# Storing three outputs of a 90-degree rotation in two halves each

## The chip, the cores and the metric

The kernel runs on one core of one Trainium2 chip. The metric is the device time of one execution in microseconds. The experiments were run in four groups on three chips, so each is set against the runs of the kernel before in its own group. "Before" and "changed" are the two kernels; where a time is quoted, it is the median of the runs.

## The reference

```python
def setup_inputs():
    return {"x": np.random.randn(8192, 8192).astype(np.float32), "k": 1}

def reference(x, k):
    return np.rot90(x, k)
```

Nothing is computed. 268 MB are read, turned by a quarter, and 268 MB are written.

## The kernel before

The input is cut into macro tiles of 1024 rows by 4096 columns. A macro tile is read by eight loads of 2 MB (128 rows each). VectorE (DVE) reverses the order of the elements inside blocks of 128, TensorE (PE) transposes 128x128 blocks into PSUM, ScalarE (ACT) copies PSUM into an output tile, and the output tile is stored (2 MB). One output needs two PSUM tiles, so two copies. There are two input buffers (`a`), two output buffers (`o`, shared with the first loads), and 68 small buffers between DVE and PE. Loads are issued by SP, stores by ACT. The last of the 16 macro tiles is cut in two tiles of 512 rows each (four loads and four outputs of 2 MB apiece), and the eight loads of these two come before their stores in the program.

```python
    def load(r0, rt, c0):
        for t in range(rt):
            ...  # a = a tile of a_pool (two buffers); some of the first eight in o_pool
            loads += 1
            nc.sync.dma_start(
                out=a[:], in_=x[r0 + t * P : r0 + (t + 1) * P, c0 : c0 + W]
            )
            ...  # eight DVE copies into tiles of r_pool (68 buffers)

    def store(r0, rt, c0, chunks, end):
        ...  # G = 4 column blocks in one output (8 in the last two tiles), PW = G / 2 in one PSUM tile
        for i, g0 in enumerate(range(0, W // P, G)):
            ...  # ot = a tile of o_pool (two buffers); in the last two tiles every other one of a_pool
            o = ot[:, : G * rows].rearrange("m (g f) -> m g f", g=G)
            S = PW if end and r0 + rows == N and g0 + G == W // P else G
            for h in range(0, G, PW):
                ...  # transposes into ps
                nc.scalar.copy(o[:, G - PW - h : G - h, :], ps)
                done = h + PW
                if done % S == 0:
                    top = M - c0 - (g0 + done) * P
                    dst = out[top : top + S * P, r0 : r0 + rows].rearrange(
                        "(g m) f -> m g f", g=S
                    )
                    nc.scalar.dma_start(out=dst, in_=o[:, G - done : G - done + S, :])
```

`S` says how many column blocks one store takes: all of the output, or half of it. Before, only the very last output is stored in halves. Numbering the outputs from 1, those of the whole macro tiles are 1 to 120, those of the last macro tile but one 121 to 124, the last ones 125 to 128.

## Time and profile before

| before | |
|---|---|
| time | 1267.97 us (6 runs, 1267.50 to 1268.66) |
| moved | 537 MB, 425 GB/s on average, 427 to 430 in most slices |
| busy | PE 55%, ACT 37%, DVE 28% |
| one store every | 9.8 us in mid run |

The first lines are from the page of the kernel before. Part 2 gives 40 slices of the span; part 3 gives for each DMA queue its packets, MB and share of the engines (q1 carries the loads, q10 the stores); part 4 is the chain of waits; part 6 lists the DMA issues with their size and time to landing.

```profile
span 1266.0 us, 10386 instructions
...
DMA  9999999999999999999999999999999999999998
GB/s 398 416 431 429 429 428 429 430 427 430 427 429 429 429 429 430 428 429 428 430 428 428 429 429 427 427 429 426 430 429 427 414 428 430 426 427 428 428 393 370
...
q10 hardware_dynamic: 18576, 268.44, 50.0%
q1 hardware_dynamic: 18432, 268.44, 49.9%
...
DMA out_dram<-ot 74%; ACT ot L147 19%; DMA a<-in_x_dram 3%; DVE ar L106 1%; ACTq L155 0%; PE pt L142 0%; ACTq L147 0%; DVEq L106 0%
...
out_dram<-ot ACTq DMA_DIRECT2D x127, 2048.0 KB, 15.9
```

The DMA is full from end to end (9 tenths or more in 39 of 40 slices). The chain names the stores, but a store takes 15.9 us to land while both queues share 428 GB/s; the first 2 MB loads, with no stores beside them, landed 4.9 us apart. No slice of the page is above 431 GB/s.

The timeline of the kernel before where the first stores start (start us, length us, engine, line, operation; ACTq is the issue of a DMA on ACT's queue, x2 are two of a kind in a row; in brackets the idle time before and what ended it):

```profile
49.65 0.65 ACTq L155 DMA_DIRECT2D out_dram<-ot  x1
...
54.16 0.55 ACTq L155 DMA_DIRECT2D out_dram<-ot  x1
...
60.89 3.64 ACT L147 COPY ot<-pt 128x2048 f32<-128x2048 f32 x2 [6.75 <-DMA out_dram<-ot]
...
64.55 0.55 ACTq L155 DMA_DIRECT2D out_dram<-ot  x1
```

The third output has to wait until the first store has landed (60.89 us), because there are two output buffers.

The same, near the end; the store at 1215.46 is that of output 120:

```profile
1205.62 0.55 ACTq L155 DMA_DIRECT2D out_dram<-ot  x1
1211.80 3.63 ACT L147 COPY ot<-pt 128x2048 f32<-128x2048 f32 x2 [6.21 <-DMA out_dram<-ot]
1215.46 0.55 ACTq L155 DMA_DIRECT2D out_dram<-ot  x1
```

The kernel before in stretches of 4 and 2 us (the last two columns are the DMA share and GB/s; in so short a stretch the figure is rough, and single ones come out above the 431 GB/s of the fullest slice of the page):

```profile
1208.00:1212.00 4.00, 2.48 (x14) 2.24 (x12) 2.77 (x8) 0.20 (x1) 0.00 (x0) 0.77 0.99 422
1212.00:1214.00 2.00, 0.28 (x2) 0.28 (x3) 0.00 (x0) 2.00 (x2) 0.00 (x0) 0.82 1.03 430
1214.00:1216.00 2.00, 2.00 (x11) 2.00 (x11) 0.00 (x0) 1.43 (x1) 0.00 (x0) 0.50 0.29 123
1216.00:1218.00 2.00, 2.00 (x17) 2.00 (x16) 0.02 (x1) 0.86 (x1) 0.00 (x0) 0.83 0.89 377
1218.00:1220.00 2.00, 1.78 (x17) 1.54 (x15) 2.00 (x6) 2.00 (x2) 0.00 (x0) 1.00 1.01 426
1220.00:1222.00 2.00, 2.00 (x21) 1.96 (x20) 0.76 (x3) 1.33 (x2) 0.00 (x0) 1.00 0.66 279
```

There is one idle stretch after 1214 us, until the store of 1215.46 starts to move, and a small one at 1221.5.

### The profile page before, as it was taken

Reading aid. Unit: us, or ns where it says so; the run is one execution under the profiler, and the core shown is the slowest. Engines: PE = TensorE matmul, PEld = TensorE weight load, DVE = VectorE, ACT = ScalarE, POOL = GpSimd, SP = SyncE. Lnnn points to the kernel's source line nnn. Section 1 sums busy time; section 2 is a strip of 40 time slices with the busy share of each in tenths; the row PEclk is TensorE's granted clock in tenths of the full one; section 3 lists DMA queues with packets and bytes.
Section 4 is the critical chain, followed back from the end, with each engine's and each line's share of the span. In section 5 each row is a group of like instructions: output and inputs, shape, how many; then the busy total and the mean of one; then the engine's idle time right before and its main releaser. Section 6 shows DMA issues by size and latency. Waiting matters only on the chain.

```text
span 1266.0 us, 10386 instructions
## 1 busy us (share of the span) xinstructions
PE 700.4 (55%) x4096; PEld 660.8 (52%) x4096; DVE 354.9 (28%) x1024; ACT 467.3 (37%) x257; POOL 0.7 (0%) x6
## 2 busy tenths in 40 slices
PE   1456455665655555555556546565464665656573
PEld 0355455554545455554555445464464654556573
DVE  4422322232222322233222322233222332223210
ACT  0333334333433334333433334333433334333364
POOL 0000000000000000000000000000000000000000
PEclk9986777777678777787777877778777667777687
DMA  9999999999999999999999999999999999999998
GB/s 398 416 431 429 429 428 429 430 427 430 427 429 429 429 429 430 428 429 428 430 428 428 429 429 427 427 429 426 430 429 427 414 428 430 426 427 428 428 393 370
DMA packets 37057, 537.55 MB, mean 425 GB/s; under 512 B 4112, under 2 KB 4112, under 8 KB 4112
## 3 DMA queue, kind: packets, MB, share of 16 engines
q10 hardware_dynamic: 18576, 268.44, 50.0%
q1 hardware_dynamic: 18432, 268.44, 49.9%
q8 instruction: 32, 0.52, 0.2%
q14 instruction: 17, 0.14, 0.0%
HBM read 268.44 MB, written 268.44 MB: 424 GB/s over the span
## 4 chain that ended last, share of the span: by engine, by line
DMA 78%; ACT 19%; issue 1%; DVE 1%; ACTq 0%; PE 0%; DVEq 0%
DMA out_dram<-ot 74%; ACT ot L147 19%; DMA a<-in_x_dram 3%; DVE ar L106 1%; ACTq L155 0%; PE pt L142 0%; ACTq L147 0%; DVEq L106 0%
## 5 line engine op out<-in xcount | busy, mean ns | idle before, releaser
L142 PE MATMUL pt<-ident,ar 128*128 128x128 f32 x4096 | 700.4, 350 | 548.3 <-ACT ot L147 465.9
L142 PEld LDWEIGHTS pt<-ident,ar 128*128 128x128 f32 x4096 | 660.8, 187 | 587.7 <-ACT ot L147 496.4
L147 ACT COPY ot<-pt 128x2048 f32<-128x2048 f32 x256 | 466.0, 1869 | 742.6 <-DMA out_dram<-ot 729.5
L106 DVE COPY ar<-a 128x512 f32<-128x512 f32 x1024 | 354.9, 420 | 865.8 <-DMA a<-in_x_dram 811.4
L147 ACT ACT_TABLE_LOAD x1 | 1.3, 1283 | 41.1 <-DVE ar L106 41.1
masks.py:199 POOL TENSOR_SCALAR_AFFINE_SELECT ident<-ident 128x128 f32<-128x128 f32 x1 | 0.3, 294 | 0.1
masks.py:197 POOL MEMSET ident<- 128x128 f32 x1 | 0.2, 205 | 0.3 <-POOLq L184 0.3
L184 POOL MEMSET const-bfloat16-1.0<- 128x1 bf16 x1 | 0.1, 102 | 0.0
L184 POOL MEMSET const-uint8-127<- 128x1 uint8 x1 | 0.1, 102 | 0.0
L184 POOL MEMSET const-float32-0.0<- 128x1 f32 x1 | 0.1, 99 | 0.2 <-issue 0.2
L184 POOL MEMSET const-float32-1.0<- 128x1 f32 x1 | 0.1, 99 | 0.0
## 6 DMA issues: line engine op xcount, KB each, us to landing
a<-in_x_dram SPq DMA_DIRECT2D x128, 2048.0 KB, 16.8
out_dram<-ot ACTq DMA_DIRECT2D x127, 2048.0 KB, 15.9
out_dram<-ot ACTq DMA_DIRECT2D x2, 1024.0 KB, 13.7
```

The lines of the kernel that those rows point to most:

```text
L106: nc.vector.tensor_copy(out=ar[:], in_=a[:, j * CH : (j + 1) * CH].rearrange("r (b m) -> r b m", m=P)[:, :, ::-1],)
L142: nc.tensor.transpose(ps[:, PW - 1 - w, t * P : (t + 1) * P], chunks[t, g * P // CH][:, g % (CH // P), :], ident,)
L147: nc.scalar.copy(o[:, G - PW - h : G - h, :], ps)
L184: nc = _bacc.Bacc("TRN2", target_bir_lowering=False, num_devices=1)
```

## The change

The intent is to let the DMA have stores sooner: the first two outputs of the first macro tile, and the first output of the last macro tile but one (outputs 1, 2 and 121), are stored in two halves, the first of them as soon as the first of the two copies is done.

```diff
-            S = PW if end and r0 + rows == N and g0 + G == W // P else G
+            starts = r0 == 0 and c0 == 0 and i < 2 or end and r0 + rows < N and i == 0
+            ends = r0 + rows == N and c0 + W == M and g0 + G == W // P
+            S = PW if starts or ends else G
```

`ends` picks the same output as the old condition. Nothing else is changed.

## The prediction

> **What bounds the kernel.** The DMA. The page gives a DMA share of 9 tenths or more in 39 of 40 slices and 427 to 430 GB/s in nearly every slice[...]. PE 55%, ACT 37% and DVE 28% are no limits. The chain of waits is 74% "DMA out<-ot" and 19% ACT copy, but that loop of two output buffers closes at the pace of the full DMA: one store per 9.8 us is 4 MB moved at 428 GB/s. 537 MB at that rate take 1254 us. So about 12 us are ramp, gaps and tail, and only a gap in the DMA can be won.
>
> **Where the DMA loses time** (stretches of 0.5 to 2 us, and the packet records):
> - start, 0 to 6 us: about 3 us, not touched;
> - 54 to 61 us, when the first two stores start: the rate falls to 279, then about 400 GB/s, while all 16 engines count as busy; the usual 0.61 us packets take up to 1.3 us. Lost: about 0.9 us of every engine. Load 9 has just ended (51.3), load 10 was issued at 50.82 but moves only from 55.4, and the first store, issued at 49.65, is the only supply: a thin queue;
> - 1214 to 1216.5 us: most engines idle up to 2.6 us, until the store issued at 1215.46; 1221.4 to 1221.9: idle 0.3 to 0.5 us, until the one issued at 1220.82;
> - end: most engines finish at 1261.7 us, one lags to 1264.4.
>
> **What the change does.** Same bytes, copies and transposes; three more stores on ACT's queue, 0.55 us of issue each (timeline).
> 1. First macro tile: the first half (1 MB) is issued at about 47.8 instead of 49.65, the second at about 50.2. It shares the DMA with load 9, which lands 1 to 2 us later (nothing urgent waits for it). The queue is less thin at 51 to 56 us. If thinness causes the slow packets, up to 0.9 us comes back; otherwise nothing. The DMA was never idle there, so an earlier store by itself wins nothing.
> 2. Last macro tile but one: the first half goes out at about 1219.0 instead of 1220.82 and fills the gap at 1221.4. But the lagging engine, which ends last, has no gap there: it ends the store before at 1224.1 and goes straight on. Less idle time of the others does not move the end. The second half and the following stores go out 0.6 us later, which the DMA's backlog hides. Value: about 0.
> 3. The gap at 1214 belongs to the output before, which is not split. It stays.
> 4. Extra ACT issue time (under 2 us in total) is off the limit.
>
> **Prediction.** 0.7 us less: 1267.3 us, range 1265.3 to 1268.8. Faster by over 2%: 0.5%; within 2%: 99%; slower: 0.5%.
>
> **What would show it.** Step 1: stretches of 54 to 62 us above 410 GB/s, packets of 0.61 us. If they still show about 280 GB/s, step 1 is wrong. Step 2: no idle at 1221.5, yet the end still set by the lagging engine. Step 3: the fall at 1214 to 1216 us unchanged. Steady state: 9.8 us per store as before.
>
> **What would make it wrong.** If the earlier first stores leave loads and stores in another order for the whole run, the spread between the DMA engines (0.4 us at the first loads, 8.5 us at the last) may grow or shrink, and the end with it by 1 to 3 us. Or the half stores delay load 10 so that a real gap opens near 60 us.

## The result, and the profile after

| | before | changed |
|---|---|---|
| median (6 runs each) | 1267.97 us | 1269.79 us |
| lowest to highest | 1267.50 to 1268.66 | 1269.65 to 1270.37 |
| time of the profiled run | 1267.83 us | 1270.37 us |

The ratio is 1.0015 (95% interval 1.0002 to 1.0027). It is the mean time of the changed kernel's runs over the mean of the other's runs of the same rounds, so it is not quite the ratio of the medians. The change costs 1.8 us: far below 2%, but clear of the noise. The profiled run of the changed kernel was its slowest, so the two profiles differ by 2.5 us.

The page of the changed kernel:

```profile
span 1268.6 us, 10387 instructions
...
GB/s 399 423 423 429 429 429 429 429 428 429 428 429 430 428 429 428 428 428 427 428 428 425 428 428 429 428 426 427 428 428 426 427 428 424 428 427 427 429 356 371
...
q10 hardware_dynamic: 19008, 268.44, 49.9%
q1 hardware_dynamic: 18432, 268.44, 49.8%
...
out_dram<-ot ACTq DMA_DIRECT2D x8, 1024.0 KB, 13.7
```

Mid run is the same. The slices that fall most are the 39th (393 to 356 GB/s), near 1220 us, and the third (431 to 423). The stores' queue has 432 more packets: each of the three outputs went out in twice as many packets of half the size, 8 KB in place of 16 KB (384 more; the other 48 are packets of 4 bytes, 16 for each store).

The timeline of the changed kernel at its first stores:

```profile
47.80 2.33 ACTq L157 DMA_DIRECT2D out_dram<-ot  x2
...
52.14 2.31 ACTq L157 DMA_DIRECT2D out_dram<-ot  x2
...
65.92 3.64 ACT L149 COPY ot<-pt 128x2048 f32<-128x2048 f32 x2 [12.04 <-DMA out_dram<-ot]
...
69.59 0.55 ACTq L157 DMA_DIRECT2D out_dram<-ot  x1
```

The first half was issued 1.85 us earlier (47.80 in place of 49.65), but the first output **landed 5 us later**: ACT may begin the third output at 65.92 us, before at 60.89.

Near the end of the changed kernel, with the store of output 120 now at 1218.78:

```profile
1210.77 0.55 ACTq L157 DMA_DIRECT2D out_dram<-ot  x1
1215.12 3.63 ACT L149 COPY ot<-pt 128x2048 f32<-128x2048 f32 x2 [4.38 <-DMA out_dram<-ot]
1218.78 0.55 ACTq L157 DMA_DIRECT2D out_dram<-ot  x1
```

The changed kernel in the same stretches:

```profile
1208.00:1212.00 4.00, 2.98 (x14) 2.98 (x15) 0.00 (x0) 2.74 (x2) 0.00 (x0) 0.50 0.48 205
1212.00:1214.00 2.00, 2.00 (x12) 2.00 (x11) 1.27 (x4) 0.00 (x0) 0.00 (x0) 0.50 1.11 467
1214.00:1216.00 2.00, 1.30 (x10) 1.06 (x9) 1.59 (x5) 0.88 (x1) 0.00 (x0) 0.92 0.94 401
1216.00:1218.00 2.00, 0.96 (x9) 0.97 (x10) 0.01 (x1) 2.00 (x2) 0.00 (x0) 1.00 0.39 164
1218.00:1220.00 2.00, 2.00 (x21) 1.96 (x19) 0.00 (x0) 1.30 (x2) 0.00 (x0) 1.00 0.12 49
1220.00:1222.00 2.00, 1.40 (x14) 1.17 (x12) 0.00 (x0) 2.00 (x2) 0.00 (x0) 1.00 1.17 492
```

There is a new hole from about 1216.7 to 1220 us, in which hardly any DMA engine works, besides an idle stretch before it (from 1208 to 1212 us the DMA share is 0.48; before it was 0.99). The packet records of the trace, which hold every packet of every queue, give the sums:

| from the packet records | before | changed |
|---|---|---|
| idle per DMA engine, 1200 to 1245 us | 2.17 us | 4.81 us |
| the last load lands (mean over the DMA engines) | 1211.8 us | 1206.6 us |
| the last packet of the run ends | 1265.1 us | 1267.6 us |
| loads minus stores, mean of 200 to 400 us | 19.8 MB | 22.1 MB |

The last row is the number of MB that the loads have moved minus those that the stores have moved; I call it the **lead** of the loads. (Here and in all runs below, a packet counts in proportion to the part of it that is done, and every trace is laid so that its first load packet starts at 2.24 us. In the timelines and stretches that packet starts at 1.75 us, so times from the packet records are about 0.5 us later than theirs.) The idle time grew by 2.64 us, and the profiled time by 2.54. That points to where the time is; it is no exact account, as e9 below shows. The lead tells when it was decided: it is 20.1 MB in both kernels at 50 us, and at 70 us it is 19.9 before and 21.7 in the changed kernel. After that it stays, in the changed kernel, for the whole run: 22.0 MB still at 1150 to 1199 us against 19.9.

So the loads get one load (2 MB) ahead of the stores in the first 25 us of stores. All loads are then done 5.2 us earlier (2.2 MB at 428 GB/s), and what is left for the last stretch is stores alone. There, as I read it, two output buffers can't feed the DMA: one store of 2 MB is gone in 4.9 us (an estimate: 2 MB at 428 GB/s), but the next has to wait for a buffer to land and for two copies of 1.87 us. Whether this hole is the loss is tested with e8.

### The profile page after: what moved, and what is told of

The parts are those of the page before. It is cut to its first block, busy times and chain, and to the rows that moved or that the text cites. A ratio compares the mean times of both kernels' runs of the same rounds, so it can differ in the third digit from the quotient of the medians.

```text
span 1268.6 us, 10387 instructions
## 1 busy us (share of the span) xinstructions
PE 714.5 (56%) x4096; PEld 680.9 (54%) x4096; DVE 364.5 (29%) x1024; ACT 466.6 (37%) x257; POOL 0.7 (0%) x6
## 4 chain that ended last, share of the span: by engine, by line
DMA 77%; ACT 20%; issue 1%; PE 1%; ACTq 0%; DVE 0%; SPq 0%
DMA out_dram<-ot 74%; ACT ot L149 20%; DMA a<-in_x_dram 3%; PE pt L144 1%; ACTq L157 0%; DVE ar L106 0%; ACTq L149 0%; SPq L101 0%
## 5 line engine op out<-in xcount | busy, mean ns | idle before, releaser
L144 PE MATMUL pt<-ident,ar 128*128 128x128 f32 x4096 | 714.5, 356 | 536.5 <-ACT ot L149 497.6
L144 PEld LDWEIGHTS pt<-ident,ar 128*128 128x128 f32 x4096 | 680.9, 191 | 569.8 <-ACT ot L149 527.7
L106 DVE COPY ar<-a 128x512 f32<-128x512 f32 x1024 | 364.5, 422 | 851.5 <-DMA a<-in_x_dram 719.6
```

The costliest lines, as they stand in the source:

```text
L106: nc.vector.tensor_copy(out=ar[:], in_=a[:, j * CH : (j + 1) * CH].rearrange("r (b m) -> r b m", m=P)[:, :, ::-1],)
L144: nc.tensor.transpose(ps[:, PW - 1 - w, t * P : (t + 1) * P], chunks[t, g * P // CH][:, g % (CH // P), :], ident,)
```

## The experiments

All runs gave correct results. Each was run in five rounds, of which one was profiled: leads, idle times and packet counts are of that one execution. (e1 and e9 start like the kernel before, and their leads came out within 0.3 MB of its own.) The kernel before ran nine times beside each group (medians 1267.94 to 1268.20 us).

**The theories.** A: the halves at the start give the loads their lead, and the lead costs the time at the end. C (rival): the split near the end costs it. Within A, two causes of the lead. A1: the DMA engines serve the two queues packet by packet; with 8 KB packets of stores against 16 KB packets of loads, the stores get one byte for two. A2: the earlier issue by itself changes the order.

A1 is so far a guess. Counting packets of both queues that start between 62 and 66 us shows whether it holds here:

| 62 to 66 us | load packets (size, GB/s) | store packets (size, GB/s) |
|---|---|---|
| before | 42 (16 KB, 172) | 62 (16 KB, 254) |
| changed | 64 (16 KB, 262) | 80 (8 KB, 164) |
| e2, start only | 73 (16 KB, 299) | 70 (8 KB, 143) |
| e4, small loads | 109 (8 KB, 223) | 100 (8 KB, 205) |
| e5, before with small loads | 72 (8 KB, 147) | 69 (16 KB, 283) |
| e6, late columns | 90 (16 KB, 369) | 92 (2 KB, 47) |

In the runs with halves the numbers of packets are equal within a quarter, whatever their sizes, from 8:1 to 1:2, and the bytes follow the sizes. In the kernel before they are not equal although the sizes are. The order of the packets tells more. The records don't name the DMA engine, but where a packet ends, another mostly starts within 5 ns; I take it to be the next one of that engine, and leave out the 8 to 35% where none or several fit. From 62 to 66 us the queue changed in 106 of 120 such steps in the changed kernel, 129 of 130 in e5, 119 of 119 in e6, and 74 of 85 in the kernel before; all 11 exceptions there were a store after a store, as if that engine had no load packet waiting, which was not shown. So here, between 62 and 66 us, the queues took turns packet by packet in 87 to 100% of these steps.

### Which of the splits? e1 and e2

e1 keeps the split near the end alone, e2 the two at the start alone:

```diff
# e1_end_only
+            starts = end and r0 + rows < N and i == 0
# e2_start_only
+            starts = r0 == 0 and c0 == 0 and i < 2
```

> Only the split in the last macro tile but one; the first macro tile as before. Theory A (the halves at the start let the loads run one load, about 2 MB, ahead of the stores, and this costs at the end): as before, 1268.0 us within 0.5; loads minus stores moved stays at 19.9 MB in mid run; the gap at 1221.5 us is filled but the end does not move. Theory C (the split near the end costs the time, by its extra store issues): about 1269.8 us, as the changed kernel.

> Only the two splits in the first macro tile; the end as before. Theory A: about 1269.8 us as the changed kernel (1269.3 to 1270.3), loads minus stores about 22 MB from 70 us to the end, and an idle stretch of about 3 us of all DMA engines near 1217 to 1220 us. Theory C: 1268.0 us.

e1: 1267.83 us, ratio 1.0000 (0.9987 to 1.0012), lead 20.1 MB, idle 2.41 us. e2: 1270.62 us (1269.54 to 1273.20), ratio 1.0022 (1.0009 to 1.0034), lead 22.0 MB, idle 4.43 us. Theory C falls. The split near the end neither wins nor costs anything that could be measured; the two at the start make the whole loss.

### A run that did not do what it should: e3

e3 should issue both halves after the second copy, to keep the small packets and take away the early issue:

```diff
+                if late and done < G:
+                    continue
+                for d in range(S, G + 1, S) if late else [done]:
                     ...  # the store of half d
```

> The first two outputs are stored in halves as in the changed kernel (8 KB packets), but both halves are issued after the second copy, so nothing is issued earlier than before; the end is not split. Theory A1 (it is the size of the store packets: 8 KB against 16 KB of the loads, so the loads move two bytes for one): loads minus stores still rises to about 22 MB and the time is 1269.3 to 1270.3 us. Theory A2 (it is the earlier issue that changes the order): loads minus stores stays near 19.9 MB and the time is 1268.0 us within 0.5.

It measured 1270.05 us (1269.78 to 1272.84) and a lead of 22.1 MB, but it tells nothing: the first half was still issued at 47.54 us. The order of the instructions was as written, but the first store did not wait for the second copy, which it does not read: ACT's queue issued it while that copy still ran (47.54 to 49.41 us):

```profile
47.54 2.44 ACTq L161 DMA_DIRECT2D out_dram<-ot  x2
```

It is a second run of e2, no more.

### Packet size against early issue: e4

e4 keeps the early halves, and makes the packets of the three loads beside them equally small, by splitting those loads (9 to 11, counted from 0; the counter has been raised by one at this place) into two halves of columns. The end is not split, so it is e2 with smaller load packets:

```diff
+            n = 2 if loads in (10, 11, 12) else 1
+            for b in range(n):
+                lo, hi = b * W // n, (b + 1) * W // n
                 nc.sync.dma_start(
-                out=a[:], in_=x[r0 + t * P : r0 + (t + 1) * P, c0 : c0 + W]
+                    out=a[:, lo:hi],
+                    in_=x[r0 + t * P : r0 + (t + 1) * P, c0 + lo : c0 + hi],
                 )
```

> The two splits at the start, and the three loads that share the DMA with them (numbers 9 to 11 from 0) are also issued in two halves of columns, so their packets are 8 KB too. The end is not split. Theory A1: the two kinds of packets are of one size again, loads minus stores comes back to about 20 MB and the time to 1268.0 us within 0.5. Theory A2: loads minus stores stays at 22 MB, the time at about 1269.8 us.

1268.63 us, ratio 1.0008 (0.9995 to 1.0022), lead 19.9 MB. Of the 1.8 us (2.6 in e2), about 0.6 are left, and they are within the noise. The timeline of e4 at the first stores:

```profile
47.71 2.45 ACTq L161 DMA_DIRECT2D out_dram<-ot  x2
...
52.24 5.16 ACTq L161 DMA_DIRECT2D out_dram<-ot  x2
61.77 3.63 ACT L153 COPY ot<-pt 128x2048 f32<-128x2048 f32 x2 [7.79 <-DMA out_dram<-ot]
```

The first half of each output is issued when the changed kernel issues it (47.80 and 52.14), but the first output has landed at 61.77 us, not at 65.92. Only the load packets were changed, though the last of the four halves went out later with them, at 56.85 in place of 53.91 us. This speaks for A1 against A2. (The later half can't be what took the lead away: in e14 below, later stores raise it.)

### The mirror: e5

e5 is the kernel before with the same three loads in small packets, and whole stores.

> The kernel before, with loads 9 to 11 issued in halves of columns (8 KB packets) and the stores whole (16 KB packets): the mirror of the change. Theory A1 (packet size sets the shares): loads minus stores falls below 19.9 MB, towards 18 MB, and stays there; then the stores are done sooner when the loads end, the idle stretch near 1214 to 1216 us shrinks, and the time is 1267.3 to 1268.0 us, little less than before because the DMA engine that ends last had no idle time. Theory A2 (only early issue of stores matters): 19.9 MB and 1268.0 us.

The lead did what A1 expects: 18.1 MB at 80 to 100 us. But it did not stay. Between 120 and 150 us the DMA lost 1.4 us against the kernel before, and the lead sprang to 20.4 MB. The time was 1271.83 us (1269.36 to 1273.57), ratio 1.0031 (1.0018 to 1.0043), not the small gain that I expected. So giving the stores too much is no remedy, and a lead need not last. Why the DMA lost that time there was not looked into further.

### Small packets without early issue: e6 and e7

e6 halves the first two outputs by columns, so that each half needs both copies; e7 halves them by partitions, which keeps 16 KB packets.

```diff
# e6_late_columns (e7: dst[b * n : (b + 1) * n] and src likewise, n = P // 2)
+                    src = o[:, G - done : G - done + S, :]
+                    for b in range(2 if starts else 1):
+                        n = rows // 2 if starts else rows
+                        nc.scalar.dma_start(
+                            out=dst[:, :, b * n : (b + 1) * n],
+                            in_=src[:, :, b * n : (b + 1) * n],
+                        )
```

> The first two outputs are stored in two halves by columns of the tile, so that each half needs both copies and none can be issued early; packets of 8 KB. Theory A1 (packet size): loads minus stores near 22 MB, time 1269.3 to 1270.5 us. Theory A2 (early issue): 19.9 MB and 1268.0 us within 0.5.

> The same, but the two halves are the two halves of the partitions, so each half needs both copies and has packets of 16 KB. Theory A1: loads minus stores near 20 MB, time 1268.0 us within 0.5. If two store instructions in place of one cost the time whatever their packets: 22 MB and 1269.3 to 1270.5 us.

e6: 1272.20 us, ratio 1.0036, lead 22.1 MB. Its packets were not 8 KB but 2 KB (the halves are not contiguous in the output tile: in the packet records a load row of 16 KB was one packet, four rows of 4 KB contiguous in the tile were one of 16 KB, two such rows one of 8 KB, and the pieces of 2 KB here one each), so it is not the test that was meant, but a stronger dose: at 65 us its lead is 23.2 MB, in the changed kernel 20.9. Its first stores were issued at 49.55, as before the change. Part of its loss is a second effect: by 100 us it had moved 1.7 us' worth of data less than the kernel before.

e7 missed: 1274.61 us, ratio 1.0057, lead 21.4 MB, the slowest of all. It is no clean test. ACT's queue needed 4.1 us for its first two issues, the second output's store went out only at 57.31 us (before 54.16), and by 60 us the DMA had lost 2.3 us. The two stores of 64 partitions were slow to issue for a reason that stays open, and they set the stores back without small packets. So a set-back had to be told apart from the packet size.

### e11, e13 and e14: the set-back told apart

e11 makes the 8 KB halves late, by a copy of one element per partition into the first half after the second copy. e13 is e11 with the small loads of e4. e14 has the one-element copies, but whole stores.

```diff
# e11_late_8k, on top of e3
                 if late and done < G:
+                    first = ps
                     continue
+                if late:
+                    nc.scalar.copy(o[:, G - PW : G - PW + 1, :1], first[:, :1, :1])
# e13_late_8k_small_loads: and the loads as in e4
# e14_late_whole: e11 with
-            S = PW if starts or ends else G
+            S = PW if ends else G
```

> The first two outputs in halves of 8 KB packets as in the changed kernel, but a copy of one element per partition into the first half, after the second copy, makes both halves wait for both copies; the end not split. Theory A1 (packet size sets the shares): loads minus stores near 22 MB in mid run, 1269.3 to 1270.8 us. Theory A2 (early issue): 19.9 MB, 1268.0 us within 0.7.

> Late halves of 8 KB packets (with the one-element copies), and loads 9 to 11 in 8 KB packets too. If the packet sizes set the lead of the loads: 20 to 20.5 MB, and 1268 to 1269 us. If the 2.6 us by which the one-element copies set back the second output set it: 22 MB and about 1271 us.

> The one-element copies after the second copy of the first two outputs, but the stores whole (16 KB packets): the set-back alone. If packet sizes set the lead: loads minus stores within 0.5 MB of 19.9, and 1268.0 to 1268.8 us. If the set-back is enough: 21 to 22 MB and about 1270 to 1271 us.

| | store packets | load packets 9 to 11 | first store, second output's store issued | lead, 200 to 400 us | time, ratio |
|---|---|---|---|---|---|
| e11 | 8 KB | 16 KB | 49.42, 56.77 | 22.1 MB | 1271.23 us, 1.0022 (1.0009 to 1.0035) |
| e13 | 8 KB | 8 KB | 49.53, 55.23 | 19.9 MB | 1269.19 us, 1.0009 (0.9995 to 1.0022) |
| e14 | 16 KB | 16 KB | 49.52, 56.86 | 20.4 MB | 1269.67 us, 1.0010 (0.9998 to 1.0023) |

ACT in e11, and then in e14 (the third output starts when the first has landed):

```profile
49.42 2.87 ACTq L164 DMA_DIRECT2D out_dram<-ot  x2
56.77 1.25 ACTq L164 DMA_DIRECT2D out_dram<-ot  x2
65.35 3.63 ACT L150 COPY ot<-pt 128x2048 f32<-128x2048 f32 x2 [8.55 <-DMA out_dram<-ot]
```

```profile
49.52 0.64 ACTq L164 DMA_DIRECT2D out_dram<-ot  x1
56.86 0.56 ACTq L164 DMA_DIRECT2D out_dram<-ot  x1
60.78 3.64 ACT L150 COPY ot<-pt 128x2048 f32<-128x2048 f32 x2 [3.95 <-DMA out_dram<-ot]
```

e11 and e14 (run on different chips) set the second output back equally (56.8 us), and differ in the halving of these stores alone, two of 8 KB packets for one of 16 KB. With 8 KB the first output lands 4.6 us later and the lead is 22.1 MB, with 16 KB it is 20.4. e13 has late halves of 8 KB and no lead. So the packet sizes set the lead; the set-back alone is worth half a MB. Nothing is issued early in e11, so early issue is not needed for the loss. This settles A1 for the lead. In time the case is weaker: e13 and e14 are not clear of the kernel before, but their medians are 1.0 and 1.5 us above it, and the interval of e14 overlaps that of e11. So something besides the lead may move the end by a microsecond; what, was not looked for.

### How little is enough: e10

> Of the three splits only the first output of the first macro tile. Theory A1: half as many small packets, so about half the lead, 20.5 to 21.3 MB, and a time between 1268.0 and 1269.8 us. If any small packet at the start tips the order for good: 22 MB and 1269.8 us.

With output 1 alone in halves the lead is 21.2 MB, and it creeps to 21.8 by 1000 to 1100 us; the time is 1270.52 us, ratio 1.0019 (1.0007 to 1.0032). The lead grew by little more than half as much at first, as A1 expects, but the time, expected between the two kernels, is that of the whole change. Two MB in small packets are enough; why the lead creeps is open.

### Is the hole at the end the loss? e8, and attempts at a better kernel: e9 and e12

e8 is the changed kernel with output 120 in halves as well; e9 is the kernel before, e12 is e4, with that split.

```diff
# e8_after_split_120 (e12 the same on top of e4)
-            ends = r0 + rows == N and c0 + W == M and g0 + G == W // P
+            ends = r0 + rows == N and g0 + G == W // P
# e9_before_split_120
-            S = PW if end and r0 + rows == N and g0 + G == W // P else G
+            S = PW if r0 + rows == N and g0 + G == W // P else G
```

> The changed kernel with one more split: the last output before the last two macro tiles (number 120), for which the DMA waits idle from about 1217 to 1220 us. Theory (the time lost is this idle stretch): its first half goes out 1.8 us earlier, near 1217.0 instead of 1218.8 us, the idle stretch shrinks by about 1.8 us, loads minus stores stays at 22 MB, and the time is 1268.0 to 1268.6 us. If the loss lies elsewhere (for example in slower packets): 1269.8 us.

> The kernel before, with output 120 in two halves: the first is issued near 1213.7 instead of 1215.5 us. In the kernel before, the DMA engine that ends last had no idle time there. If that engine sets the end: 1267.6 to 1268.2 us although the idle stretch of the others shrinks by 1.8 us. If the idle time of the others counts: 1266.2 to 1266.8 us.

> The kernel with the two splits at the start and small packets for loads 9 to 11 (which gained 0.6 us at the start and lost it near 1215 us), and with output 120 in two halves. Theory: the idle stretch near 1213 to 1217 us shrinks, and the time is 1267.0 to 1268.0 us, the best of all; if the lagging DMA engine sets the end, 1268.0 to 1268.7 us.

e8: 1268.31 us, ratio 1.0005 (0.9991 to 1.0019). The issue of output 120 in e8, and its stretches:

```profile
1215.06 3.63 ACT L149 COPY ot<-pt 128x2048 f32<-128x2048 f32 x2 [3.78 <-DMA out_dram<-ot]
1216.95 2.32 ACTq L157 DMA_DIRECT2D out_dram<-ot  x2
```

```profile
1216.00:1218.00 2.00, 1.02 (x9) 1.03 (x10) 0.00 (x0) 2.00 (x2) 0.00 (x0) 1.00 0.68 287
1218.00:1220.00 2.00, 2.00 (x20) 1.96 (x19) 0.00 (x0) 1.30 (x2) 0.00 (x0) 1.00 0.95 389
```

The first half is out at 1216.95 in place of 1218.78, the hole is nearly closed (389 GB/s where the changed kernel had 49), the idle time per engine is 3.23 in place of 4.81 us, and 1.5 of the 1.8 us have come back, with the lead still at 22.1 MB. The same split in the kernel before wins nothing (e9), so it undoes the loss and is no gain of its own. By the medians, then, most of the loss comes through the hole at the end. That the lead costs nothing besides is not shown: the interval of e8 reaches to 1.0019, and it overlaps that of the changed kernel.

e9: 1268.15 us, ratio 1.0000 (0.9987 to 1.0014). I expected less idle time and the same end; the end was the same, but the idle time was not less (3.25 us): the hole at 1214 us closed, and one of about 2 us opened at 1220 to 1222 us, before the next store. So e9 says nothing about which DMA engine sets the end, and it shows that the idle time is no exact measure of the loss. e12: 1269.20 us, ratio 1.0006 (0.9994 to 1.0019), no gain. No kernel here beats the kernel before.

## Why the prediction was wrong

The range ended at 1268.8 us; the time is 1269.79. Point by point:

- *The DMA is the bound; an earlier store by itself wins nothing.* Right. The first store packet starts at 51.7 to 51.8 us by the packet records (51.2 to 51.3 in the time of the timelines) in the kernel before and in the changed kernel alike, whether the store was issued at 49.65 or at 47.80: until then the engines were still moving load 9. Why the store issued at 47.80 did not take turns with load 9 sooner is open.
- *Step 1, up to 0.9 us comes back at the first stores.* Partly right. From 54 to 62 us the DMA ran at 373 GB/s before and 420 in the changed kernel (means of two stretches of 4 us; the changed kernel's second one, 391, is under the 410 that was asked for). Its packets were no longer slow: none took over 0.85 us there, before up to 1.39. At 70 us the changed kernel was ahead by 0.6 us' worth of data. By 100 us that was gone; in e2, with the same start, 0.4 us stayed.
- *"It shares the DMA with load 9, which lands 1 to 2 us later (nothing urgent waits for it)."* This is the step that failed. Load 9 did land 1.4 us later (its last part at 54.29 in place of 52.88 us), but it was the wrong overlap to look at: the stores shared the DMA mainly with loads 10 and 11. There, in halves, they have packets of half the size and get little more than half the bytes of the loads while both are queued (164 against 262 GB/s from 62 to 66 us). Load 10 landed 3.8 us earlier (63.85 in place of 67.68), the first output 5 us later (65.92 in place of 60.89), and the loads kept a lead of 2 MB. I had taken "Same bytes" to mean that halves are neutral for the DMA.
- *Step 3, the gap at 1214 us stays.* Wrong, as a consequence. The fall at 1214 to 1216 us is gone (401 GB/s, before 123), and two others came, at 1208 to 1212 and from 1216.7 to 1220 us. The idle time per engine near the end grew from 2.17 to 4.81 us. By e8, the second one makes most of the cost.
- *Step 2, the split near the end is worth nothing; step 4, the extra issues are off the limit.* The value is right: e1 has 1267.83 us. The reason given for step 2, the lagging engine, is not shown; e9 was meant to test it and did not.
- *Steady state 9.8 us per store.* Right: 9.76 us in the changed kernel (stores issued at 1190.99 and 1200.75).
- *What would make it wrong.* The text named "loads and stores in another order for the whole run", but it looked for the effect in the spread between the DMA engines. That did not grow (the last load landed over 8.6 us before, and over 8.1 us in the changed kernel). The lead of the loads was the thing to watch.

## What to carry to other kernels

When loads and stores compete for the DMA engines, compare the sizes of their packets: here the two queues took turns packet by packet (106 of 120 steps), so halving one side's packets took bandwidth from it while both were queued (164 against 262 GB/s), although its transfers were still of 1 MB. An advantage that one side gains at the start can stay until the end in a pipeline whose DMA is full (22 MB from 70 us on in the changed kernel; in e5 it was lost by 150 us), so look at the place where one side runs out to see what it costs. And before splitting a store to start it earlier, check in the trace when its first packet moves, not when it is issued.
